# A decoder layer with product-key experts: all 128 lower tokens get their first products by gathered rows, 12 chunks of `u` are loaded beside the queries, and index look-ups go to 16 bits

## The chip, the cores and the metric

The kernel runs on one NeuronCore of a Trainium2 chip. The metric is the device time of one execution in microseconds (us), as the median over several runs. Engines are named as in the profile: PE is TensorE's matmul, PEld its weight load, DVE is VectorE, ACT is ScalarE, POOL is GpSimd, SP is SyncE, which here only issues transfers.

## The reference, cut to what matters

The layer normalises `x` (256 tokens of 1024), projects it, runs two attention branches, merges them and adds the result to `x`. Behind that stands the part that the change touches, PEER, a product-key expert retrieval. With `h2 = RMSNorm(x)` it computes, in words and symbols:

```
q      = h2 @ w_q                      # 8 heads, two halves of 128 each
s1, s2 = q halves @ sub_keys           # 128 scores each, per head
top 16 of s1, top 16 of s2             # 256 sums, of which the best 16 are kept
expert = 128 * i1 + i2                 # one of 16384
gate   = softmax(the 16 best sums)
out   += sum over 8 heads x 16 experts of gate * gelu(h2 . u[expert]) * v[expert]
```

`u` and `v` are tables of 16384 rows of 1024 float32 numbers, 64 MB each. A token uses 128 of the rows.

## The kernel before, in words

Tokens 128 to 255 (the upper ones) and part of the lower ones take their expert products densely: every row of `u` is multiplied with every such token, and a matrix of gates that is zero for experts not chosen selects. The other lower tokens have their 128 rows of `u` fetched by index and dotted on DVE.

**Projections.** All projections go through a list of pieces of 128x2x512 weights. SP loads them (`L191`) into a ring of 6 buffers, `raw_ring`; ACT (`L137`) and DVE (`L138`) cut each into a high and a low part, `rhi` and `rlo`; PE multiplies three combinations (`L219` to `L221`, `L228` to `L230`). The last 16 pieces are those of `w_q`, the queries stage. `pump()` advances the waiting epilogues by a step after each piece.

**Early turns.** While the projections run, `early_turns` loads a few chunks of `u` (a chunk is 128 rows), transposes them on DVE in blocks of 32 (`L682`) and stores them in DRAM as `turned`. `NPRE` of them, each eighth chunk, are later loaded ready-made; the others are transposed on PE (`L666`) and copied out by ACT (`L667`).

**The residual's epilogue** (`L510` to `L558`) makes `h2` and its transposes in `hTf`, of which `NA` columns are used. On POOL's queue it copies the rows of `NX` lower tokens to DRAM (`h2x`, `L553`), and from there to `h2y` (`L556`), where each row stands 8 times, once for each head. `h2r` tiles are loaded from `h2y` by `rows_x` at the start of the u stage.

**Queries.** `queries` (`L560`) evicts a piece's product (ACT `L564`), multiplies with the sub-keys (`L573`) and puts a `topk` generator on the chain. `topk` (`L821` to `L900`) runs on DVE in steps, paid from a budget (`BUDGET_Q` beside a piece, `BUDGET` beside a chunk). Its last part finds the expert numbers: a compare of `iota` with `tf` (`L853`), a multiply with `ce` (`L856`) and a reduce (`L857`), each over 128x864 numbers; then `ef` becomes `ei`, and the gates follow, normalised in `L889` to `L891`.

**The u stage** runs over 128 chunks (`L1122`): load of the next chunk on SP (`L621`, or `L642` for a turned one), transposes two chunks ahead, 8 matmuls against `hTf` of `NA` columns (`L1137`), and beside each chunk `GATHER` gather steps and a piece of the chain. A gather step fetches one row of `u` per partition by an indirect transfer on POOL (`L924`, four buffers) and dots the row that came three steps before on DVE (`dot_v`, `L935`). The first 64 of these are those of the 64 tokens that were always gathered (`h`), the other `NU` - 64 those of the `NX` extra tokens (16 for each of `NXG` groups, with `h2r` as the other operand). When the chain of the upper tokens is done, `dense_gates` (`L1040`) comes: `columns(1)` (`L1045`) transposes the indices and gates of the upper tokens on PE, then for four tokens at a time DVE makes one-hot rows (`L1025`, `L1026`), ACT scales them (`L1030`), PE multiplies (`gp`, `L1064`) and DVE and ACT write the result into `W` (`L1077`, `L1079`). `W` holds 128 chunks by `ND` = 192 tokens; its columns 0 to 87 (`SCRATCH`) serve as scratch or lie unused until the products arrive there.

**The V stage** (`L1174`) multiplies `W` with the table `v`, and gathers what belongs to the 64 tokens (`GATHER_V`).

All queues are in order, and the order is that in which the program is written. `load_to` issues a load on SP a fixed number of pieces or chunks ahead; a load waits until its ring buffer is free.

Of the kernel before, what the change touches and what calls it, by code (L numbers as in the profile page):

```python
# [11 lines left out]
F32 = mybir.dt.float32  # L12
F32R = mybir.dt.float32r
BF16 = mybir.dt.bfloat16
I32 = mybir.dt.int32
U32 = mybir.dt.uint32
AF = mybir.ActivationFunctionType
# [11 lines left out]
NG = 64  # L29
ND = S - NG  # L30
NXP = 16
NXG = 3
NX = NXP * NXG
NA = ND - NX
RING = 4
GATHER_V = 0.5
GATHER = 0.95
RAWS = 6
AHEAD = 4
TAHEAD = 2  # L40
# [3 lines left out]
LAG_G = 2  # L44
SCRATCH = 88
TOPK = 16
NPRE = 15
STEP = 8
PRE0 = 20
WARM = 8  # L50
# [14 lines left out]
def layer_kernel(ctx, tc, x, mix_norm_g, w_in, ret_w_branch, moba_q_gain, moba_k_gain, moba_w_branch,  # L65
# [444 lines left out]
    def residual(j):  # L510
        def epi(o):

            xg = []
            for t in range(NT):
                c = slice(512 * j, 512 * (j + 1))
                V.tensor_tensor(xt[:, t, c], xt[:, t, c], o[t], op=OP.add)
            for t in range(NT):
                c = slice(512 * j, 512 * (j + 1))
                a = t2([P, 512], "xg")
                V.tensor_tensor(a, xt[:, t, c], grow2[:, c], op=OP.mult)  # L520
                sq = t2([P, 512], "sq2")
                A.activation(sq, xt[:, t, c], AF.Square, accum_out=ss2[:, j, t:t + 1])
                xg.append(a)
            yield
            yield
            for t in range(NT):
                p = side()
                for c in range(4):
                    T.transpose(p[:, c * P:(c + 1) * P], xg[t][:, c * P:(c + 1) * P], ident)
                split_to(qk_h[j][:, :, t * P:(t + 1) * P], qk_l[j][:, :, t * P:(t + 1) * P],  # L530
                         p.rearrange("p (c q) -> p c q", c=4))
            if j == 0:
                return
            nc.gpsimd.dma_start(x1d, xt)  # L534
            V.tensor_tensor(ss2[:, 0], ss2[:, 0], ss2[:, 1], op=OP.add)
            V.tensor_scalar(ss2[:, 0], ss2[:, 0], 1.0 / D, EPS, op0=OP.mult, op1=OP.add)
            G.tensor_tensor(r2, ss2[:, 0], minus_half[:, :NT], op=OP.pow)
            yield
            V.scalar_tensor_tensor(h2, xt[:, 0, :], r2[:, 0:1], grow2, op0=OP.mult, op1=OP.mult)
            hn = t4([P, D], "hn2")  # L540
            V.scalar_tensor_tensor(hn, xt[:, 1, :], r2[:, 1:2], grow2, op0=OP.mult, op1=OP.mult)
            yield
            for src, t0, n0, n in ((h2, NG, P, NA - P), (hn, 0, 0, P)):
                for q in range(2):
                    k = slice(4 * q, 4 * q + 4)
                    p = side()
                    for c in range(4):
                        T.transpose(p[:, c * P:(c + 1) * P], src.rearrange("p (i k) -> p k i", k=KC)[:, 4 * q + c], ident)
                    pv = p.rearrange("p (c q) -> p c q", c=4)[:, :, t0:t0 + n]
                    A.activation(hTf[:, k, n0:n0 + n], pv, AF.Copy)  # L550
                yield

            nc.gpsimd.dma_start(h2x, h2[P - NX:])  # L553
            nc.gpsimd.dma_start(h2[NG:], h2[:NG])
            yield
            nc.gpsimd.dma_start(h2y, h2x.rearrange("(n i) d -> n i d", n=NXG)[:, None].to_broadcast([NXG, H, NXP, D]))  # L556
            yield
        return epi  # L558

    def queries(q):  # L560
# [67 lines left out]
    def load_any(i):  # L628
# [8 lines left out]
            load(i)  # L637
        elif i < len(pieces) + NK:
            c = i - len(pieces)
            if c % STEP == STEP - 1 and c // STEP < NPRE:  # L640
                u_raw[c] = raw_tile()
                nc.sync.dma_start(u_raw[c], turned[c // STEP])  # L642
            else:
                u_raw[c] = load_rows(peer_u, c)
        elif i < len(pieces) + 2 * NK:
            v_raw[i - len(pieces) - NK] = load_rows(peer_v, i - len(pieces) - NK)
# [174 lines left out]
    def topk(t, q, s_sb):  # L821
# [11 lines left out]
        cand = []  # L833
        for n0, src in ((6400, v), (6528, xf)):
            dst = scratch[:, n0:n0 + 2 * NCAND].rearrange("p (h n) -> p h n", h=2)
            for (i, a, b), n in zip(CAND, COFF):
                V.tensor_tensor(dst[:, :, n:n + a * b].rearrange("p h (a b) -> p h a b", a=a),
                                src[:, 1, :, None, :b].to_broadcast([P, 2, a, b]),
# [4 lines left out]
        ts_ = tk.tile([P, 2, TOPK], F32, name="ts_")  # L843
        ti = tk.tile([P, 2, TOPK], U32, name="ti")
        tf = tk.tile([P, 2, TOPK], F32, name="tf")
        ef = tk.tile([P, 2, TOPK], F32, name="ef")
        for _ in top16([(ts_[:, h, :], ti[:, h, :], cs[:, h, :], tmp[h][:, :NCAND]) for h in range(2)]):
            yield 0.55
        V.tensor_copy(tf, ti)
        yield 0.85  # L850
        for h in range(2):
            oh = scratch[:, 5120:5120 + TOPK * NCAND].rearrange("p (k n) -> p k n", k=TOPK)
            V.tensor_tensor(oh, iota[:, None, :NCAND].to_broadcast([P, TOPK, NCAND]),  # L853
                            tf[:, h, :, None].to_broadcast([P, TOPK, NCAND]), op=OP.is_equal)
            yield 0.9
            V.tensor_tensor(oh, oh, ce[:, h, None, :].to_broadcast([P, TOPK, NCAND]), op=OP.mult)  # L856
            V.tensor_reduce(ef[:, h, :], oh, axis=AX.X, op=OP.add)  # L857
            yield 1.9
        sl = slice(2 * q * TOPK, 2 * (q + 1) * TOPK)
        e1 = ef.rearrange("p h k -> p (h k)")  # L860
# [108 lines left out]
    def gather_step():  # L969
# [21 lines left out]
        if gs["sum"] < gs["v"] and (gs["v"] - gs["sum"] == RING or gs["v"] == NJ):  # L991
# [6 lines left out]
                V.scalar_tensor_tensor(gs["acc"], r, av[:, j:j + 1], gs["acc"], op0=OP.mult, op1=OP.add)  # L998
            gs["sum"] += 1

    for i in range(n_mixer + 3, len(pieces)):
        load_to(i + 1)
        cut(i + 3)
        products(i)
        pump()
# [1 line left out]

    while tasks:  # L1010
        pump()
    cps.close()
# [266 lines left out]
```

## Time and profile before

| | |
|---|---|
| median of 3 runs | 1034.11 us (1033.67 to 1040.05) |
| the profiled execution | 1033.85 us, its span 1031.8 us |
| granted TensorE clock, mean | 0.992 |
| PE busy | 1005.6 us, 97% of the span |
| DVE, ACT, POOL busy | 815.1, 546.1, 307.0 us |
| queries stage ends, u stage begins | about 332 us |
| DMA traffic | 301.43 MB, mean 292 GB/s |

The profile is one execution. A row of a list of waits says which engine at which line waited for what: us in total, times, longest. A row of the chain of waits gives a start, a duration and what the time went to. A row of a timeline gives start, duration, engine, line, operation, out<-in, and in brackets the idle time before. [...]

### The profile page before, as it was taken

The numbers are of one execution on the slowest core, as the hardware profiler recorded it, in microseconds if no ns is written. First come the engines' busy times: TensorE is split into PE (matmuls) and PEld (weight loads), VectorE is DVE, ScalarE is ACT, GpSimd is POOL, SyncE is SP. The second block draws the span as 40 slices with busy tenths as digits, with TensorE's granted clock in tenths as the row PEclk, the third lists the DMA queues.
The fourth block names the chain that finished last, engine by engine and source line by source line (L and its number), as shares of the span: only waits on it lengthen the run. The fifth ranks groups of instructions, "written<-read, shape, count | busy, mean of one in ns | idle before, by whom it ended". The sixth has DMA issues, their size and how long they took to land.

```text
span 1031.8 us, 19502 instructions
## 1 busy us (share of the span) xinstructions
PE 1005.6 (97%) x7384; PEld 967.9 (94%) x7384; DVE 815.1 (79%) x1482; ACT 546.1 (53%) x991; POOL 307.0 (30%) x256
## 2 busy tenths in 40 slices
PE   8999999999949999999999999999999999999997
PEld 6887998997949999999999999999999999999997
DVE  6567667978548895699977999994788888888887
ACT  5545544534524434443346776679655555555553
POOL 2421000000102344444443443542433333333330
PEclk9999999999969999999999999999999999999999
DMA  9775787987735999899999787887799999999993
GB/s 332 194 201 169 235 247 212 301 269 225 239 123 162 383 372 352 330 367 373 376 384 344 280 284 255 285 320 244 270 345 345 352 336 345 348 343 345 341 347 108
DMA packets 103067, 301.43 MB, mean 292 GB/s; under 512 B 10740, under 2 KB 21005, under 8 KB 102822
## 3 DMA queue, kind: packets, MB, share of 16 engines
q1 hardware_dynamic: 64732, 186.07, 52.1%
q0 software_dynamic: 27008, 96.82, 26.0%
q10 hardware_dynamic: 11234, 17.31, 5.4%
q8 instruction: 58, 0.95, 0.4%
q14 instruction: 35, 0.29, 0.1%
HBM read 289.15 MB, written 12.00 MB: 292 GB/s over the span
## 4 chain that ended last, share of the span: by engine, by line
PE 89%; DMA 3%; DVE 3%; ACT 2%; issue 1%; ACTq 0%; POOL 0%; DVEq 0%; POOLq 0%
PE acc L1137 24%; PE acc L1170 19%; PE turn L666 10%; PE acc L1171 8%; PE gp L1064 4%; PE acc L228 3%; PE acc L229 3%; PE acc L230 3%; PE acc L219 3%; PE acc L220 3%; PE acc L221 3%; DMA raw_ring<-in_peer_w_q_dram 2%; PE side L573 1%; PE side L349 1%; PE side L374 1%
## 5 line engine op out<-in xcount | busy, mean ns | idle before, releaser
L924 POOL DMA_INDIRECT rows<-in_peer_u_dram,eg x112 | 140.0, 1250 | 130.0 <-DVE rows L935 50.4
L924 POOL DMA_INDIRECT rows<-in_peer_v_dram,eg x64 | 106.8, 1669 | 168.3 <-DVE vacc L998 167.4
L666 PE MATMUL turn<-ident,raw_ring 128*128 128x128 f32 x904 | 118.5, 274 | 0.8 <-ACT W L577 0.8
L666 PEld LDWEIGHTS turn<-ident,raw_ring 128*128 128x128 f32 x904 | 110.0, 191 | 1.0 <-ACT W L577 1.0
L935 DVE SCALAR_TENSOR_TENSOR rows<-rows,h 128x1024 f32<-128x1024 f32 x64 | 78.4, 1229 | 8.6 <-DMA rows<-in_peer_u_dram,eg 8.5
L998 DVE SCALAR_TENSOR_TENSOR vacc<-rows,av,vacc 128x1024 f32<-128x1024 f32 x63 | 80.6, 1279 | 0.0
L1108 ACT ACTIVATE cw<-W 128x384 fp32r<-128x384 f32 x64 | 33.7, 526 | 81.9 <-PE acc L1171 31.7
L1109 DVE TENSOR_TENSOR cw<-W,cw 128x384 fp32r<-128x384 f32 x64 | 36.3, 568 | 33.7 <-ACT cw L1108 33.7
L1079 ACT ACTIVATE W<-gp 128x512 f32<-128x512 f32 (+18 forms) x48 | 27.5, 577 | 41.4 <-DVE W L1077 35.0
L1030 ACT ACTIVATE oh_buf<-oh_buf,tT 128x128 f32<-128x128 f32 x128 | 40.9, 407 | 0.4 <-DVE oh_buf L1026 0.4
L1077 DVE TENSOR_TENSOR W<-gp,W 128x328 f32<-128x328 f32 (+17 forms) x36 | 36.5, 1015 | 5.3 <-PE gp L1064 5.0
L1094 POOL TENSOR_TENSOR W<-W,gl 128x288 f32<-128x288 f32 (+17 forms) x24 | 15.6, 651 | 83.9 <-ACT gl L1093 77.8
L935 DVE SCALAR_TENSOR_TENSOR rows<-rows,rlo__3191 128x1024 f32<-128x1024 f32 x16 | 19.4, 1217 | 21.1 <-DMA rows<-in_peer_u_dram,eg 21.0
L1064 PE MATMUL gp<-oh_buf 128*128 128x128 f32 x256 | 33.8, 276 | 0.0
L1137 PE MATMUL acc<-hTf,raw_ring 128*128 128x144 f32 x240 | 31.9, 286 | 0.0
L1064 PEld LDWEIGHTS gp<-oh_buf 128*128 128x128 f32 x256 | 31.5, 191 | 0.1
L1137 PEld LDWEIGHTS acc<-hTf,raw_ring 128*128 128x128 f32 x240 | 30.3, 190 | 0.0
L534 POOL DMA_DIRECT2D x1d<-xt x1 | 0.7, 652 | 91.7 <-DMA raw_ring<-in_peer_w_q_dram 91.7
L1025 DVE TENSOR_TENSOR oh_buf<-niota,tT 128x512 f32<-128x512 f32 x32 | 22.1, 690 | 7.0 <-PE gp L1064 6.4
L144 POOL TENSOR_TENSOR gny<-va,minus_half 128x8 f32<-128x8 f32 x2 | 3.3, 1653 | 79.1 <-DVE va L436 79.1
L935 DVE SCALAR_TENSOR_TENSOR rows<-rows,rlo__3252 128x1024 f32<-128x1024 f32 x16 | 19.3, 1218 | 9.4 <-DMA rows<-in_peer_u_dram,eg 9.4
L1026 DVE TENSOR_TENSOR oh_buf<-iota,tT 128x512 f32<-128x512 f32 x32 | 25.4, 793 | 0.0
(2091 smaller groups left out, 3491.2 us busy)
## 6 DMA issues: line engine op xcount, KB each, us to landing
raw_ring<-in_peer_v_dram SPq DMA_DIRECT2D x128, 512.0 KB
raw_ring<-in_peer_u_dram SPq DMA_DIRECT2D x113, 512.0 KB
raw_ring<-in_w_in_dram SPq DMA_DIRECT2D x52, 512.0 KB
raw_ring<-in_peer_w_q_dram SPq DMA_DIRECT2D x16, 512.0 KB
raw_ring<-turned SPq DMA_DIRECT2D x15, 512.0 KB
eraw<-in_peer_u_dram ACTq DMA_DIRECT2D x32, 128.0 KB
turned<-eT ACTq DMA_DIRECT2D x8, 512.0 KB
raw_ring<-in_ret_w_branch_dram SPq DMA_DIRECT2D x8, 512.0 KB
```

The lines of the kernel that those rows point to most:

```text
L666: T.transpose(p[:, k * P:(k + 1) * P], r.rearrange("p (i k) -> p k i", k=KC)[:, 4 * q + k], ident)
L924: G.indirect_dma_start(out=r, out_offset=None, in_=tab, in_offset=bass.IndirectOffsetOnAxis(ap=eg[:, j:j + 1], axis=0))
L935: V.scalar_tensor_tensor(r, r, 1.0, h, op0=OP.mult, op1=OP.mult, accum_out=av[:, j:j + 1])
L998: V.scalar_tensor_tensor(gs["acc"], r, av[:, j:j + 1], gs["acc"], op0=OP.mult, op1=OP.add)
L1030: A.activation(o1[:, j], o1[:, j], AF.Copy, scale=tT[:, t, 2, k + j:k + j + 1])
L1064: T.matmul(p[:, j * P:(j + 1) * P], o2, o1, start=True, stop=True)
L1077: V.tensor_tensor(w[:, :, :c], p[:, :, :c], w[:, :, :c], op=OP.mult)
L1108: A.activation(w[:, :, :ND], W[:, c:c + 2, :], AF.Copy)
L1109: V.tensor_tensor(w[:, :, ND:], W[:, c:c + 2, :], w[:, :, :ND].bitcast(F32), op=OP.subtract)
L1137: T.matmul(pa[:, n:n + NA], uT[:, k * P:(k + 1) * P], hTf[:, k], start=(c % 2 == 0 and k == 0), stop=(k == KC - 1), skip_group_check=True)
L1170: T.matmul(o[b][:, :2 * ND], vh[:, n], w, start=(c == 0), stop=False, skip_group_check=True)
L1171: T.matmul(o[b][:, :ND], vl[:, n], w[:, :ND], start=False, stop=(c == NK - 1), skip_group_check=True)
```

## The change

Five edits. `NXG` goes from 3 to 4, so all lower tokens gather their first products: `NX` 48 to 64, `NU` 112 to 128, `NA` 144 to 128 columns of `L1137`, and `GATHER` 0.95 to 1.08. Twelve chunks of `u` (0, 1, 2, 8, 14, ... 56) are loaded by `hold` beside the queries' pieces into unused columns of `W`, and `load_any` skips them later. `h2y` is written by four copies with 16 rows outermost instead of one copy with 24. The expert look-up's `ce`, `oh` and `ef` become 16-bit integers. `NPRE` goes from 15 to 14. The rest of the text keeps the line numbers of the kernel before; in the changed kernel they are a few higher.

```diff
-NXG = 3
+NXG = 4
 NX = NXP * NXG
 NA = ND - NX
...
-GATHER = 0.95
+GATHER = 1.08
...
-NPRE = 15
+HELD = [0, 1, 2] + list(range(8, 62, 6))
+HELD0 = 20
+NPRE = 14
...
             for src, t0, n0, n in ((h2, NG, P, NA - P), (hn, 0, 0, P)):
-                for q in range(2):
+                for q in range(2 if n else 0):
...
-            nc.gpsimd.dma_start(h2y, h2x.rearrange("(n i) d -> n i d", n=NXG)[:, None].to_broadcast([NXG, H, NXP, D]))
-            yield
+            for n in range(NXG):
+                src = h2x[NXP * n:NXP * (n + 1)]
+                nc.gpsimd.dma_start(h2y[n].rearrange("h i d -> i h d"), src[:, None, :].to_broadcast([NXP, H, D]))
+                yield
...
             c = i - len(pieces)
+            if c in HELD:
+                return
...
             dst = scratch[:, n0:n0 + 2 * NCAND].rearrange("p (h n) -> p h n", h=2)
+            if src is xf:
+                dst = tk.tile([P, 2, NCAND], I16, name="ce", bufs=2)
...
-        ef = tk.tile([P, 2, TOPK], F32, name="ef")
+        ef = tk.tile([P, 2, TOPK], I16, name="ef")
...
-            oh = scratch[:, 5120:5120 + TOPK * NCAND].rearrange("p (k n) -> p k n", k=TOPK)
+            oh = scratch[:, 5120:5120 + TOPK * NCAND // 2].bitcast(I16).rearrange("p (k n) -> p k n", k=TOPK)
...
+    def hold():
+        n0, c = 1024 * (len(HELD) - len(held)), held.pop(0)
+        u_raw[c] = W[:, HELD0:SCRATCH, :].rearrange("p c t -> p (c t)")[:, n0:n0 + D]
+        nc.sync.dma_start(u_raw[c], peer_u[0, c * P:(c + 1) * P, :])
+
     for i in range(n_mixer + 3, len(pieces)):
         load_to(i + 1)
+        if held and i > n_mixer + 3:
+            hold()
...
+    while held:
+        hold()
```

On SP's queue the queries stage stood so before: the loads of `w_q`, with two of the sub-keys between, then the first chunks of `u`.

```order
L191 DMA raw_ring<-in_w_out_dram 128x2x512 x8
L191 DMA raw_ring<-in_peer_w_q_dram 128x2x512 x5
L632 DMA raw_ring<-in_peer_sub_keys_dram 128x8x128 x2
L191 DMA raw_ring<-in_peer_w_q_dram 128x2x512 x11
L621 DMA raw_ring<-in_peer_u_dram 128x1024 x7
L642 DMA raw_ring<-turned 128x1024
```

After the change, from the sub-keys on (`L1016` is `hold`; the lines left out alternate one `w_q` load and one held load):

```order
L637 DMA raw_ring<-in_peer_sub_keys_dram 128x8x128 x2
L194 DMA raw_ring<-in_peer_w_q_dram 128x2x512 x4
L1016 DMA W<-in_peer_u_dram 128x1024
L194 DMA raw_ring<-in_peer_w_q_dram 128x2x512
...
L1016 DMA W<-in_peer_u_dram 128x1024 x4
L626 DMA raw_ring<-in_peer_u_dram 128x1024
L1016 DMA W<-in_peer_u_dram 128x1024
L626 DMA raw_ring<-in_peer_u_dram 128x1024 x3
L649 DMA raw_ring<-turned 128x1024
```

Of the last seven `w_q` loads each has a held load ahead of it, and five more held loads stand behind, among the first chunks; the ring's first three chunks fall away, since chunks 0 to 2 are held.

POOL's queue around the residual's epilogue, before:

```order
L534 DMA x1d<-xt 128x2048
L537 TENSOR_TENSOR r_75<-ss_116,minus_half 128x2
L553 DMA h2x<-h_74 48x1024
L554 DMA h_74<-h_74 64x1024
L556 DMA h2y<-h2x 24x1x16384
L867 DMA eg<-ei 64x16
L924 DMA rows<-in_peer_u_dram,eg 128x1024 x5
```

and in the changed kernel:

```order
L537 DMA x1d<-xt 128x2048
L540 TENSOR_TENSOR r_75<-ss_116,minus_half 128x2
L556 DMA h2x<-h_74 64x1024
L557 DMA h_74<-h_74 64x1024
L561 DMA h2y<-h2x 16x8x1024 x4
L877 DMA eg<-ei 64x16
L934 DMA rows<-in_peer_u_dram,eg 128x1024 x6
```

The one copy of 24 runs of 16384 numbers becomes four of 16x8 runs of 1024, and one gather more stands before the next copy of indices.

DVE just before the second `L891`, the end of the upper tokens' chain, before (`rlo__3252` is the third `h2r`, and `rows` is a gathered row):

```order
L853 TENSOR_TENSOR W<-iota,tf 128x864
L856 TENSOR_TENSOR W<-W 128x864
L857 TENSOR_REDUCE ef<-W 128x16
L935 SCALAR_TENSOR_TENSOR rows,av<-rows,rlo__3252 128x1024 x2
...
L879 TENSOR_TENSOR gates<-ts__5209 128x32
L935 SCALAR_TENSOR_TENSOR rows,av<-rows,rlo__3252 128x1024 x5
L889 TENSOR_REDUCE sm<-gates 128x8
L890 RECIPROCAL sm<-sm 128x8
L891 TENSOR_TENSOR gates<-gates,sm 128x128
```

and after (`rlo__3277` is the fourth `h2r`):

```order
L862 TENSOR_TENSOR W<-iota,tf 128x864
L865 TENSOR_TENSOR W<-W,ce 128x864
L867 TENSOR_REDUCE ef<-W 128x16
L945 SCALAR_TENSOR_TENSOR rows,av<-rows,rlo__3249 128x1024 x2
...
L889 TENSOR_TENSOR gates<-ts__5232 128x32
L945 SCALAR_TENSOR_TENSOR rows,av<-rows,rlo__3249 128x1024 x2
L945 SCALAR_TENSOR_TENSOR rows,av<-rows,rlo__3277 128x1024 x4
L899 TENSOR_REDUCE sm<-gates 128x8
L900 RECIPROCAL sm<-sm 128x8
L901 TENSOR_TENSOR gates<-gates,sm 128x128
```

One more dot stands in this stretch; over the whole stage 80 dots stand ahead of this last line, where there were 70. On PE `columns(1)` stays where it was, behind the products of 79 chunks.

## Rows read from the trace of the kernel before

**Rows 1.** The page: span, and busy time of each engine (busy us, share, instructions).

```profile
span 1031.8 us, 19502 instructions
PE 1005.6 (97%) x7384; PEld 967.9 (94%) x7384; DVE 815.1 (79%) x1482; ACT 546.1 (53%) x991; POOL 307.0 (30%) x256
```

**Rows 2.** The list of PE's waits from 0 to 340 us, its largest item.

```profile
PE side L573 <- ACT W L564: 13.1, 1, 13.1
```

**Rows 3.** ACT's timeline at 295.75 us, and the chain of waits from 275 us on (start, us, what). Between 302.47 and 304.60 stand eleven matmuls of 0.21 us.

```profile
295.75 1.06 ACT L137 ACTIVATE rhi__2735<-raw_ring 128x1024 fp32r<-128x1024 f32 x1 [15.16 <-DMA raw_ring<-in_peer_w_q_dram]
...
275.24 21.74 DMA raw_ring<-in_peer_w_q_dram
...
298.68 3.78 PE side L573 x16
302.47 0.21 PE acc L228
...
304.60 0.21 PE acc L229
...
305.93 0.12 PE acc L230
...
315.08 0.71 PE side L573 x4
315.79 1.60 PE side L573 x12
```

**Rows 4.** Windows of 4 us in the queries stage.

```profile
core 0: us, PE busy (x) PEld busy (x) DVE busy (x) ACT busy (x) POOL busy (x), PEclk, DMA share, GB/s
...
282.00:286.00 4.00, 3.62 (x31) 3.42 (x29) 0.17 (x1) 0.00 (x0) 0.00 (x0) 1.00 0.35 144
286.00:290.00 4.00, 0.00 (x0) 0.00 (x0) 0.00 (x0) 0.00 (x0) 0.00 (x0) 0.71 0.14 55
290.00:294.00 4.00, 0.00 (x0) 0.00 (x0) 0.00 (x0) 0.00 (x0) 0.00 (x0) 0.50 0.26 84
294.00:298.00 4.00, 0.00 (x0) 0.00 (x0) 1.16 (x2) 1.97 (x2) 0.00 (x0) 0.50 0.43 160
```

**Rows 5.** DMA queues from 286 to 294 us: packets, MB, share of 16 engines.

```profile
q0 software_dynamic: 8, 0.39, 11.7%
```

**Rows 6.** Windows of the u stage (columns as in rows 4).

```profile
332.00:397.00 65.00, 64.97 (x546) 64.97 (x547) 58.68 (x199) 28.40 (x56) 26.84 (x25) 1.00 0.98 377
397.00:433.00 36.00, 36.00 (x305) 36.00 (x305) 14.46 (x51) 17.94 (x33) 14.88 (x19) 1.00 0.85 310
433.00:532.00 99.00, 99.00 (x834) 99.00 (x833) 94.98 (x326) 39.27 (x81) 41.82 (x35) 1.00 0.99 378
532.00:550.00 18.00, 18.00 (x153) 18.00 (x152) 8.50 (x19) 10.44 (x19) 7.83 (x8) 1.00 1.00 387
550.00:690.00 140.00, 140.00 (x1198) 140.00 (x1198) 132.87 (x193) 99.30 (x301) 62.16 (x58) 1.00 0.82 293
```

**Rows 7.** Lists of the waits of DVE and of POOL from 335 to 550 us, the largest of each.

```profile
DVE rows L935 <- DMA rows<-in_peer_u_dram,eg: 38.6, 18, 10.7
...
POOL rows L924 <- DVE rows L935: 50.4, 26, 5.0
```

**Rows 8.** DMA from 332 to 550 us, all packets.

```profile
DMA packets 22272, 80.02 MB, mean 367 GB/s; under 512 B 2669, under 2 KB 2829, under 8 KB 22247
```

**Rows 9.** Timelines of DVE (first two rows) and PE (last row) around 546 us.

```profile
544.83 1.23 DVE L935 SCALAR_TENSOR_TENSOR rows<-rows,rlo__3252 128x1024 f32<-128x1024 f32 x1 [1.39 <-DMA rows<-in_peer_u_dram,eg]
...
546.53 0.29 DVE L891 TENSOR_TENSOR gates<-gates,sm 128x128 f32<-128x128 f32 x1
...
550.19 0.38 PE L1045 MATMUL turn<-ident,i12f 128*128 128x128 f32 x2
```

**Rows 10.** The view of the one line `L682`: count, shortest/median/longest in ns, and the longest wait for it.

```profile
L682 DVE STREAM_TRANSPOSE eT<-eraw x16: 1107/1156/1218, 82.5 to 238.8; 128x512 f32<-128x512 f32 x16
...
  ACT rhi__1677 L137: 2.1, 1
```

**Rows 11.** The chain of waits in the u stage, before the gates (first two) and in the gate part (last).

```profile
503.68 0.89 PE turn L666 x8
504.57 1.96 PE acc L1137 x16
...
560.12 0.89 PE gp L1064 x8
```

**Rows 12.** Groups of DVE instructions by line from 332 to 728 us (count | busy us, mean ns of one), and the first dot's row of DVE's timeline.

```profile
L935 DVE SCALAR_TENSOR_TENSOR rows<-rows,rlo__3252 128x1024 f32<-128x1024 f32 x16 | 19.3, 1218 | 9.4 <-DMA rows<-in_peer_u_dram,eg 9.4
L1077 DVE TENSOR_TENSOR W<-gp,W 128x328 f32<-128x328 f32 (+17 forms) x36 | 36.5, 1015 | 5.3 <-PE gp L1064 5.0
L857 DVE TENSOR_REDUCE ef<-W 128x16 f32<-128x864 f32 x14 | 14.7, 1053 | 0.5
L856 DVE TENSOR_TENSOR W<-W 128x864 f32<-128x864 f32 x13 | 13.7, 1056 | 0.2
L837 DVE TENSOR_TENSOR W<-txf 128x16 f32<-128x16 f32 (+3 forms) x30 | 3.3, 177 | 0.0
...
335.59 1.22 DVE L935 SCALAR_TENSOR_TENSOR rows<-rows,h 128x1024 f32<-128x1024 f32 x1
```

**Rows 13.** Windows of DVE's `L935` alone: length, DVE busy (x counts two records for each dot), PEclk, DMA share, GB/s.

```profile
433.00:532.00 99.00, 43.76 (x72) 1.00 0.99 378
```

More of the change, by code (lines that the diff above doesn't have):

```diff
@@ L14 @@
 BF16 = mybir.dt.bfloat16
+I16 = mybir.dt.int16
 I32 = mybir.dt.int32
@@ L856, in topk @@
             V.tensor_tensor(oh, oh, ce[:, h, None, :].to_broadcast([P, TOPK, NCAND]), op=OP.mult)
-            V.tensor_reduce(ef[:, h, :], oh, axis=AX.X, op=OP.add)
+            with nc.allow_low_precision("one term of each sum is not zero, an integer below 2 ** 14"):
+                V.tensor_reduce(ef[:, h, :], oh, axis=AX.X, op=OP.add)
             yield 1.9
@@ L999, in gather_step @@
             gs["sum"] += 1
+    held = list(HELD)
+    def hold():
+        n0, c = 1024 * (len(HELD) - len(held)), held.pop(0)
+        u_raw[c] = W[:, HELD0:SCRATCH, :].rearrange("p c t -> p (c t)")[:, n0:n0 + D]
+        nc.sync.dma_start(u_raw[c], peer_u[0, c * P:(c + 1) * P, :])
     for i in range(n_mixer + 3, len(pieces)):
         load_to(i + 1)
+        if held and i > n_mixer + 3:
+            hold()
         cut(i + 3)
```

## The prediction

> **What bounds the kernel now.** The page comes first: TensorE is busy for 1005.6 of a span of 1031.8 us [rows 1]. So time can go only where PE's own work shrinks or where PE waits. The list of PE's waits up to the end of the queries stage holds one large item, 13.1 us for ACT's `L564` [rows 2]. From 332 to 690 us PE is busy in every us of every window at a granted clock of 1.00 [rows 6]: the u stage is bound by PE's instructions.
>
> The stall, followed back: ACT's cut `L137` sat 15.16 us until a piece of `w_q` landed, and the chain of waits has that transfer from 275.24 on, for 21.74 us [rows 3]. Meanwhile the DMA engines were mostly idle: shares 0.35, 0.14, 0.26, 0.43 in the four windows from 282 us [rows 4]. What ran between 286 and 294 us was on POOL's queue, q0: 8 packets, 0.39 MB, 11.7% of the engines [rows 5], some 49 KB a packet. That is `h2y<-h2x`, whose rows of 16384 elements are 64 KB each. My reading: the `w_q` load is spread over all engines and is done only when its last part is, and a few engines sit behind long packets. The stall also costs clock: granted 0.50 from 290 to 298 us [rows 4]. The first `L573` group behind it took 3.78 us where the next took 0.71 + 1.60, and 11 matmuls took 0.21 instead of 0.12 [rows 3]: 1.5 + 1.0 = 2.5 us.
>
> In the u stage DVE and POOL have waits that PE does not see: DVE 38.6 us for gathered rows, POOL 50.4 for DVE to free a row buffer [rows 7]. The DMA engines stand at 0.98 to 1.00 there save in one stretch at 0.85 [rows 6], moving 80.02 MB from 332 to 550 at a mean of 367 GB/s [rows 8]. That matters because of one meeting point: PE's `columns(1)` (`L1045`) transposes `i12f` and `gates`, which the last DVE `L891` of the token half completes. DVE ended it at 546.53 + 0.29 = 546.82; PE came at 550.19 and did not wait [rows 9]. The slack is 3.4 us. An edit that makes PE earlier by more than that turns into a wait, unless DVE gets there earlier too.
>
> **The change, part by part.** The sum is made against the profiled run's own 1033.85 us, 0.3 below the median of 1034.11.
>
> *Early turns, 15 to 14.* One pair of DVE transposes of 1156 ns goes, and with it a wait like the 2.1 us that ACT spent on one [rows 10]; PE is paced there by the cuts. Between 0 and -2; I take -1.0. Chunk 119 is then turned on PE: 8 transposes, 0.89 us [rows 11], +0.9.
>
> *Row copies.* Four copies of 16x8x1024 put 4 KB packets on 16 rows. If they spread, the stall goes: -13.1, with its clock -2.5. Bounds 0 to -15.6. [...]
>
> *Held loads.* 12 loads of 0.524 MB are 6.3 MB, at 387 GB/s [rows 6] 16.3 us of DMA time, interleaved on SP with the `w_q` loads. Between 282 and 298 us the engines have room for about 70% of that [rows 4], and `w_q` itself would land earlier. Bounds 0 to +16 (all in front of the pieces that PE needs); I take +1, as the engines' free share is the nearest row.
>
> *Short matmuls.* A chunk's 16 steps take 1.96 us with 144 moving columns; 16 `gp` steps with 128 columns of the same type take 2 x 0.89 = 1.78 [rows 11]. That is -0.18 a chunk, x128 = -23.0. PE has no idle time to absorb it. Upper bound 0, if another engine paces the stage.
>
> *All lower tokens gathered.* 16 more rows and 16 more dots `L935` of 1.22 us [rows 12] on DVE. By the order of instructions 80 u dots, where 70 stood, come before the `L891` that PE waits for, while `columns(1)` stays behind 79 chunks. PE gets there 79 x 0.18 = 14.2 us sooner in the stage: 550.19 - 332.03 = 218.2 becomes 204. DVE got there at 214.8. What will it need now? By bytes: 12 loads less are -6.3 MB, 10 or 11 rows more +5.5, one more `h2r` +0.5: the same 80 MB through engines that were full. So about 215 again; at the 387 GB/s of the best window all the way it is 207, and I allow 222 for later row buffers. **A new wait of PE, 215 - 204 = 11 us** (3 to 18), and behind it the same clock loss as behind the 13.1: +2.5.
>
> *Gate part (550 to 690).* DVE is busy for 132.87 of 140 [rows 6]. GATHER 1.08 adds 0.13 x 38 chunks = 5 dots, 6 us; 32 evictions `L1077` of 1015 ns instead of 36 [rows 12] take 4 back, and PE's steps get 0.18 us shorter while DVE's work a step does not. +3, between 0 and +6.
>
> *16 bits.* The multiply costs 1056 ns and the reduce 1053, 13 and 14 of them after 332 us [rows 12]. No row has them in 16 bits. Nearest below is an elementwise operation on 128x16, 177 ns [rows 12]; a conversion could cost as much again. So a gain of 0 to 0.88 us each; I take 0 for the sum. Whatever it saves first lengthens DVE's wait for rows (cover 38.6 us); without that cover the 13 multiplies at half time would be 6.9 us. [...]
>
> Sum: 1033.85 - 1.0 + 0.9 - 13.1 - 2.5 + 1.0 - 23.0 + 11.0 + 2.5 + 3.0 = 1012.7, **1013 us**. With the wait between 3 and 18, own range 1005 to 1020.
>
> **The rivals.**
> A. *DVE keeps up, no wait at `columns(1)`*: 1013 - 13.5 = 999. For it: the stretch at DMA share 0.85 is slack, and the held chunks lie at the front, where they let the gathers run ahead. Against it: POOL and DVE wait on each other there [rows 7], and the engines are full otherwise.
> B. *The gathers keep their pace per dot.* The first dot began at 335.59, the 70th at 544.83 [rows 9, 12]: 209.24 / 69 = 3.03 us each. 80 of them then end the chain at 3.6 + 79 x 3.03 + 2.0 = 245 us, the wait is 41, and the time 1013 + 30 = 1043, slower than before. It decides at 2.92 us a dot, where the wait is 32. For it: the ring of four row buffers and POOL's 50.4 us. Against: from 433 to 532 us 36 dots took 99 us, 2.75 each [rows 13], and those had more chunk loads beside them.
> C. *The stall stays in another form*: small copies that are mostly overhead, or held loads ahead of `w_q`. +15.6: 1028. For it: 6.3 MB are added to the very window. Against: the idle shares.
> D. *The 16-bit multiplies run at half time and DVE is the bound*: 13 x 0.53 = 6.9 us off the new wait, and the clock loss stays: 1006. Against: DVE waits for rows, so its time is not what ends last.
>
> **How the numbers follow.** Chances: the forecast 0.46, A 0.18, B 0.09, C 0.12, D 0.10, others 0.05. The likeliest gives 1013. The range runs from 997 (A, with a gate part at 0 instead of +3) to 1032 (C with the longer wait); outside lie B and a tail of A, under 2 in 10. One per cent, 10.3 us, is about what a measurement can tell from no change: 1023.8 and 1044.5 are the bounds. The forecast, A and D are faster, 0.74, less a few hundredths for a wait near 20 us and half of the others: 0.69. C and most of B lie within 1%: 0.26. Slower is B's upper half: 0.05.
>
> **What would show it.** Right: no `L573` wait above 2 us, the windows 282 to 298 with shares near 1; 16 `L1137` steps in 1.78; a PE wait of about 11 us at `columns(1)` on `gates`; an unchanged 0.98 DMA share up to it. Wrong: PE waiting at `u` loads instead (held chunks late, or gathers crowding them), a wait for `w_q` of 10 us or more, or `L856` still at 1.05 with DVE as the last to end. A result under 1003 means A; one above 1025 means B or C, told apart by where PE waits.

## The result, and the profile after

The changed kernel takes 1029.38 us, the median of 20 runs, against 1034.17 us before: a ratio of 0.9947, with an interval of 0.9929 to 0.9965. That is half a per cent faster, where 2% had been forecast (1013 us, range 997 to 1032). The profiled execution took 1025.9 us. Its runs scatter from 1022 to 1033 us, those of before from 1032 to 1040; two of the changed kernel's, at 1040 and 1041 us, more than 1.5% above its fastest, are left out of this range and of the ratio.

The page's first lines, and PE's list of waits over the whole span (us in total, times, longest):

```profile
span 1024.1 us, 19561 instructions
PE 989.0 (97%) x7384; PEld 950.7 (93%) x7384; DVE 822.9 (80%) x1508; ACT 547.3 (53%) x989; POOL 319.8 (31%) x278
...
PE acc L1158 <- ACT rhi__5491 L674: 12.7, 1, 12.7
PE gp L1085 <- ACT oh_buf L1051: 4.1, 5, 1.6
PE turn L1066 <- DVE gates L901: 3.6, 1, 3.6
PE side L578 <- ACT W L569: 2.5, 2, 2.2
```

PE's busy time fell by 16.6 us [rows 1]. The stall in the queries stage went from 13.1 [rows 2] to 2.5 us in two waits, the longer of 2.2, and a new one of 12.7 + 3.6 us stands in the u stage. First the queries stage, in windows of 4 us (columns as in rows 4: busy us of each engine and its instructions, TensorE's granted clock as a share of full speed, the mean busy share of the 16 DMA engines, GB/s):

```profile
278.00:282.00 4.00, 4.00 (x36) 4.00 (x35) 3.11 (x15) 1.06 (x1) 0.00 (x0) 1.00 1.01 392
282.00:286.00 4.00, 1.85 (x13) 1.64 (x12) 3.33 (x17) 2.03 (x3) 0.00 (x0) 0.92 1.04 405
286.00:290.00 4.00, 4.00 (x26) 4.00 (x25) 1.09 (x11) 1.87 (x3) 0.00 (x0) 0.66 1.04 396
```

The DMA engines stand at 1.01 to 1.04 where they stood at 0.14 to 0.43 [rows 4]. The u stage begins at the first transpose of a held chunk, 317.6 us, and not at 332.0:

```profile
L673 PE MATMUL turn<-ident,W x96: 272/274/375, 317.6 to 458.5; 128*128 128x128 f32 x96
```

Now the new stall. ACT's timeline shows where PE's wait of 12.7 us comes from: ACT reached the `Exp` of the upper tokens' gates (`L896`) and stood 16.67 us for DVE's `L889` there, and the copies `L674` of transposed chunks, which PE needs, are queued behind it.

```profile
511.46 1.28 ACT L896 ACT_TABLE_LOAD   x1
529.41 0.31 ACT L896 ACTIVATE gates<-gates 128x128 f32<-128x128 f32 x1 [16.67 <-DVE gates L889]
529.63 1.07 ACT L674 ACTIVATE rhi__5491<-turn 128x512 f32<-128x512 f32 x2
```

The chain of waits goes on from there to `columns(1)` and out into the gate part:

```profile
519.65 7.61 DMA rows<-in_peer_u_dram,eg
...
527.29 1.23 DVE rows L945 x2
...
529.63 0.95 POOL rows L934
...
532.87 5.78 DMA rows<-in_peer_u_dram,eg
...
538.74 1.23 DVE rows L945 x2
...
540.44 0.30 DVE gates L901
...
540.78 0.33 PE turn L1066
541.11 1.42 PE turn L673 x8
542.53 2.90 PE acc L1158 x16
...
549.87 1.79 PE acc L1158 x16
```

This is a loop: a row lands, DVE dots it, the free buffer lets POOL issue the next row, and that one lands 6 to 8 us later. The norm `L901` ends at 540.74, which is 223.1 us behind the stage's start (214.8 before, [rows 9]). And 16 matmuls take 1.79 us, not 1.96 [rows 11]. PE's clock shows what the wait cost besides:

```profile
522.00:526.00 4.00, 0.00 (x0) 0.00 (x0) 3.75 (x5) 0.00 (x0) 2.45 (x2) 0.50 1.03 409
526.00:530.00 4.00, 0.00 (x0) 0.00 (x0) 3.86 (x11) 0.59 (x2) 2.17 (x2) 0.50 0.53 206
530.00:534.00 4.00, 3.74 (x17) 3.74 (x18) 2.90 (x6) 3.34 (x6) 3.39 (x3) 0.50 0.85 264
534.00:538.00 4.00, 3.21 (x27) 2.97 (x25) 2.17 (x3) 1.36 (x3) 2.33 (x3) 0.94 0.87 290
538.00:542.00 4.00, 1.22 (x8) 1.22 (x9) 3.50 (x10) 0.72 (x2) 1.87 (x2) 0.92 0.89 338
542.00:546.00 4.00, 4.00 (x26) 4.00 (x25) 3.90 (x8) 2.32 (x7) 2.95 (x3) 0.66 0.72 231
```

PE's timeline has the first 16 matmuls behind the wait of 12.7 us take 3.78 us, where the 16 ahead of it took 1.95, and the 8 transposes after them 1.37 and not 1.05, which is 2.15 us lost. Behind the second wait the chain above shows 1.42 and 2.90 us for what later takes 0.89 (8 transposes) and 1.79, another 1.64.

From `columns(1)` to the first matmul of the V stage 182.0 us pass, where it was 178.8 before. The V stage itself takes 301.3 and 302.6 us.

### The profile page after: what moved, and what is told of

It reads as the page before. It is cut to its first block, busy times and chain, and to the rows that moved or that the text cites. A ratio compares the mean times of both kernels' runs of the same rounds, so it can differ in the third digit from the quotient of the medians.

```text
span 1024.1 us, 19561 instructions
## 1 busy us (share of the span) xinstructions
PE 989.0 (97%) x7384; PEld 950.7 (93%) x7384; DVE 822.9 (80%) x1508; ACT 547.3 (53%) x989; POOL 319.8 (31%) x278
## 4 chain that ended last, share of the span: by engine, by line
PE 60%; DMA 14%; DVE 12%; issue 6%; POOL 4%; ACT 3%; POOLq 0%; DVEq 0%; SPq 0%; ACTq 0%
PE acc L1191 20%; DMA rows<-in_peer_u_dram,eg 11%; PE acc L1192 9%; DVE rows L945 5%; PE acc L231 4%; PE acc L233 4%; PE acc L232 4%; PE acc L222 4%; PE acc L223 3%; PE acc L224 3%; POOL rows L934 3%; PE acc L1158 3%; PE gp L1085 1%; DVE W L1098 1%; PE turn L673 1%
## 5 line engine op out<-in xcount | busy, mean ns | idle before, releaser
L934 POOL DMA_INDIRECT rows<-in_peer_u_dram,eg x128 | 150.7, 1177 | 127.4 <-DVE rows L945 50.1
L934 POOL DMA_INDIRECT rows<-in_peer_v_dram,eg x64 | 102.4, 1599 | 170.3 <-DVE vacc L1008 164.8
L673 PE MATMUL turn<-ident,raw_ring 128*128 128x128 f32 x816 | 108.2, 276 | 0.7 <-ACT rhi__6709 L674 0.7
L673 PEld LDWEIGHTS turn<-ident,raw_ring 128*128 128x128 f32 x816 | 99.5, 191 | 0.9 <-ACT rhi__6709 L674 0.9
L1100 ACT ACTIVATE W<-gp 128x512 f32<-128x512 f32 (+16 forms) x48 | 30.7, 643 | 36.1 <-DVE W L1098 32.9
L1115 POOL TENSOR_TENSOR W<-W,gl 128x256 f32<-128x256 f32 (+15 forms) x24 | 17.9, 746 | 79.3 <-ACT gl L1114 73.1
L1098 DVE TENSOR_TENSOR W<-gp,W 128x328 f32<-128x328 f32 (+15 forms) x32 | 31.8, 993 | 0.9 <-PE gp L1085 0.5
L1158 PE MATMUL acc<-hTf,raw_ring 128*128 128x128 f32 x224 | 28.5, 282 | 0.0
L1158 PEld LDWEIGHTS acc<-hTf,raw_ring 128*128 128x128 f32 x224 | 27.4, 200 | 0.0
```

What stands on the lines that cost most here:

```text
L673: T.transpose(p[:, k * P:(k + 1) * P], r.rearrange("p (i k) -> p k i", k=KC)[:, 4 * q + k], ident)
L934: G.indirect_dma_start(out=r, out_offset=None, in_=tab, in_offset=bass.IndirectOffsetOnAxis(ap=eg[:, j:j + 1], axis=0))
L1098: V.tensor_tensor(w[:, :, :c], p[:, :, :c], w[:, :, :c], op=OP.mult)
L1158: T.matmul(pa[:, n:n + NA], uT[:, k * P:(k + 1) * P], hTf[:, k], start=(c % 2 == 0 and k == 0), stop=(k == KC - 1), skip_group_check=True)
```

## The experiments

"Chain end" is the end of the second `L901` (in the kernel before `L891`), counted from the first transpose of the u stage: 214.8 us before, 223.1 in the whole change. Times are medians. Edits are against the changed kernel.

**Without the fourth group.**

```diff
-NXG = 4
+NXG = 3
-GATHER = 1.08
+GATHER = 0.95
```

> The change without its fourth group of gathered tokens: NXG 3 and GATHER 0.95 as before, so 144 columns and 70 dots ahead of the upper tokens' last norm, with the held chunks, the small copies, the 16-bit look-ups and NPRE 14 kept. Theory S (supply: in the u stage the gathered rows come through full DMA engines, the chain of the upper tokens ends when its rows have landed, and the whole gain of the short matmuls is handed back as PE's wait and as a DVE-bound gate part): the front keeps its 14.4 us, no wait at the Exp or at columns(1), PE's pitch stays at 1.96 for 16 matmuls; 1018 to 1021 us, so faster than the whole change at 1029. Theory F (the fourth group still pays on balance, some 5 to 10 us, and the loss lies elsewhere): slower than the whole change, 1034 to 1039.

Measured: 1016.71 us, ratio 0.9836 (0.9823 to 0.985); chain end 209.4, no wait there. So the other four edits alone bring 17 us, and the fourth group, as it was put in, costs 12.7 us on balance. Theory F falls; S's time was 1.3 us too high.

**No held chunks.**

```diff
-HELD = [0, 1, 2] + list(range(8, 62, 6))
+HELD = []
```

> The whole change with no held chunk: all 12 are loaded in the u stage again, which puts 6.3 MB more ahead of columns(1). Theory S: the upper tokens' chain ends 15 to 18 us later behind the stage's start (at 357 GB/s), PE's wait there grows from 16 to 30 us or more, and the time is 1040 to 1047 us. Theory D (DVE's own work and the hand-over of four row buffers set the end of the chain, not bytes): the wait stays at 16 us and the time at 1027 to 1031. In both the queries stage keeps its gain, or gains 1 to 2 us.

Measured: 1037.36 us, ratio 1.004 (1.0024 to 1.0055); chain end 232.3, and PE waits 21.2 + 2.9 us. The 6.3 MB matter, but for 9 us and not for the 15 to 18 that bytes over a full engine would give. Theory D falls, and S is too strong.

**GATHER back at 0.95.**

```diff
-GATHER_V = 0.5
+GATHER_V = 0.7
-GATHER = 1.08
+GATHER = 0.95
```

> The whole change with GATHER back at 0.95, so 70 dots instead of 80 stand ahead of the upper tokens' last norm, and about 10 of the 64 tokens' own rows are dotted in the V stage, whose GATHER_V goes from 0.5 to 0.7 to take them in. Theory S: 5.2 MB less ahead of columns(1), the chain ends about 208 us behind the stage's start where PE comes at 204, the wait is 0 to 5 us, the clock is not lost, and the time is 1008 to 1016 us. If the gate part is what DVE bounds whatever stands ahead of it (theory G): the wait goes but the gate part grows, 1020 to 1027.

Measured: 1002.36 us (996.9 to 1003.3), ratio 0.9694 (0.9681 to 0.9707). Chain end 206.8, PE waits 1.0 us for it, and the part from there to the V stage takes 172.0 us and not 182.0. Ten dots fewer ahead of the norm are worth 27 us, more than S had said, since the gate part recovers too.

**Half of each chunk loaded.**

```diff
-        nc.sync.dma_start(r, tab[0, c * P:(c + 1) * P, :])
+        n = P // 2 if tab is peer_u else P
+        nc.sync.dma_start(r[:n], tab[0, c * P:c * P + n, :])
```

> The whole change with each chunk of u that is loaded into the ring in the u stage cut to its first 64 rows; the other half of the buffer keeps old numbers, so the products of half the experts are left out. Instructions on every engine stay the same; 15 MB less ahead of columns(1). Theory S: the chain ends near 181 to 195 us behind the stage's start, no wait of PE at the Exp or at columns(1), and 1006 to 1013 us. Theory D: DVE is busy for 181 us of its 223 there whatever the loads do and the row buffers go round as before, the wait stays above 10 us, 1024 to 1030.

Measured: 1060.75 us, ratio 1.026 (1.0227 to 1.0293), chain end 252.8: both expectations missed. The DMA queues from 340 to 520 us (packets, MB, share of 16 engines), of this run, and then of the whole change:

```profile
q0 software_dynamic: 8147, 28.20, 54.8%
q1 hardware_dynamic: 5315, 17.92, 39.7%
```

```profile
q0 software_dynamic: 9445, 32.94, 48.5%
q1 hardware_dynamic: 8766, 31.94, 45.7%
```

A packet on q1 took on average 0.397 x 16 x 180 us / 5315 = 215 ns, against 0.457 x 16 x 180 / 8766 = 150; on q0 194 against 148. With loads into 64 partitions the mean packet of both queues was slower in this run, those of the rows too; why, no run shows. As a test of bytes the run is spoilt; it does show that PE's wait (35.2 us) follows the rows' landing with DVE's instructions unchanged.

**Odd chunks not loaded.** The clean form of the same test.

```diff
+            elif c % 2 and c - 1 in u_raw and c - 1 not in HELD:
+                u_raw[c] = u_raw[c - 1]
```

> The whole change, but of two neighbouring chunks of u the odd one is not loaded where its even neighbour was: it takes the neighbour's buffer, so its experts' products are wrong and 11.5 MB (22 chunks of 128 whole rows) are missing ahead of columns(1). Unlike the cut to 64 rows, where each 4 KB packet took some 215 ns in place of 150, the packets stay as they are. Theory S (bytes over full DMA engines set when the upper tokens' chain ends): it ends 191 to 200 us behind the stage's start, PE does not wait, 1005 to 1012 us. Theory D (DVE's own work sets it): the end stays at 220 or more, 1026 to 1031. Theory M (the first 60 us are DVE's, the rest is supply): 205 to 213, a wait of 2 to 8 us, 1011 to 1020.

Measured: 1011.83 us, ratio 0.9786 (0.9768 to 0.9804); chain end 216.2, PE waits 5.6 + 3.9 us. The DMA engines stood at 0.92 in the stage's first 62 us, at 0.77 in the next 40 and at 0.93 to 0.94 in the 100 behind, so they had room, and still the chain ended only 7 us sooner. S and D fall.

**Half dots.**

```diff
-        V.scalar_tensor_tensor(r, r, 1.0, h, ...
+        V.scalar_tensor_tensor(r[:, :D // 2], r[:, :D // 2], 1.0, h[:, :D // 2], ...
```

> The whole change with each dot of a gathered row over 512 of its 1024 numbers: half of each first product of the lower tokens is left out, and a dot takes some 0.69 us in place of 1.22. Bytes and the order are the same. Theory S: the chain still ends 215 to 223 us behind the stage's start, the wait of PE there is 11 us or more, and only the gate part gains: 1018 to 1026. Theory D: 80 dots less 0.53 us are 42 us, the chain ends well before PE, 1002 to 1009. Theory M: the end at 205 to 214, 1008 to 1017.

Measured: 1011.71 us, ratio 0.9793 (0.9774 to 0.9813); chain end 216.1, PE waits 5.9 + 2.6 us. So 11.5 MB less and 30 us of DVE's work less (it is busy for 133.7 of the stage's first 202 us, and for 163.8 in the whole change) are worth the same 7 us of the chain's end. Neither resource alone sets it. DVE's waits for rows grew from 36.4 to 65.2 us in those 202 us: most of what the dots gave up went into waiting. M named these times, but put the chain's end 2 to 3 us too early, and its reason, one bound after the other, does not fit: each relief helps a little. My reading is that of a loop whose steps follow one another; it led to theory L below.

**Look-ups in 32 bits.**

```diff
-            if src is xf:
-                dst = tk.tile([P, 2, NCAND], I16, name="ce", bufs=2)
-        ef = tk.tile([P, 2, TOPK], I16, name="ef")
+        ef = tk.tile([P, 2, TOPK], F32, name="ef")
...
-            oh = scratch[:, 5120:5120 + TOPK * NCAND // 2].bitcast(I16)...
+            oh = scratch[:, 5120:5120 + TOPK * NCAND]...
```

> The whole change with the look-ups in 32 bits as before; the multiply then takes 1056 ns again and not 607, 13 to 14 times in the u stage, 6 us in all, most of them ahead of the upper tokens' norm. Theory S: DVE waits that much less for rows, the chain ends where it did, 1027 to 1031. Theory D: 5 to 6 us later, 1033 to 1036.

Measured: 1034.83 us (12 runs), ratio 1.0007 (0.999 to 1.0024); chain end 232.4. Against the change's 1029.38 that is 5.4 us, as theory D had it: the look-ups' time (13 x 0.449 = 5.8 us) comes through although DVE waits for rows for 36.4 us of the stage's first 202 in the change and for 38.1 here. In the whole change the multiply takes 607 ns in place of 1056 [rows 12], and the reduce is as it was:

```profile
L867 DVE TENSOR_REDUCE ef<-W 128x16 int16<-128x864 int16 x14 | 14.7, 1053 | 0.5
...
L865 DVE TENSOR_TENSOR W<-W,ce 128x864 int16<-128x864 int16 x13 | 7.9, 607 | 0.2
```

**One copy for `h2y`.**

```diff
-            for n in range(NXG):
-                src = h2x[NXP * n:NXP * (n + 1)]
-                nc.gpsimd.dma_start(h2y[n].rearrange("h i d -> i h d"), src[:, None, :]...
-                yield
+            nc.gpsimd.dma_start(h2y, h2x.rearrange("(n i) d -> n i d", n=NXG)[:, None]...
+            yield
```

> The whole change with h2y written by one copy again, now of 32 runs of 16384 numbers. If the 64 KB packets on few DMA engines were what held up w_q: the stall at the sub-keys' products comes back with 13 us or more and its clock loss, the u stage starts 14 to 20 us later, 1043 to 1050. If the held loads or the order of the queue had removed it: 1027 to 1032.

Measured: 1046.17 us, ratio 1.014 (1.0112 to 1.0169). The old stall is back at its old size, and the u stage begins at 328.9 us:

```profile
PE side L576 <- ACT W L567: 13.1, 1, 13.1
```

So the form of the copies removed it; without the held chunks it stayed away as well (u stage at 315.0). The packets in the trace show which form: in this run 32 packets of 64 KB follow one another four at a time, most of them 2.4 us long, and in the kernel before 24 of them three at a time. That is as many side by side as there are groups (`NXG`), so my reading is that the groups stand outermost in the one copy, and not its 24 or 32 runs. The four copies changed two things at once, the 4 KB packets and the 16 rows outermost; no run tells them apart.

**A fifth row buffer.** `tk`, a pool of tiles, has room for one.

```diff
-RING = 4
+RING = 5
...
-        tag = "hh" if j % 2 else "hl"
-        r = hp_.tile([P, D], F32, name="rows", tag=tag, bufs=2)
+        n = gs["n"] = gs.get("n", -1) + 1
+        tag = ("hh", "hl", "hh", "hl", "r5")[n % 5]
+        r = tk.tile([P, D], F32, name="rows", tag=tag) if tag == "r5" else hp_.tile(...)
```

> The whole change with a fifth row buffer, so that four gathered rows are on their way where there were three. Nothing else changes but that a dot comes one gather step later (79 in place of 80 ahead of the norm). Theory L (loop: a row takes some 8.0 to 8.3 us from issue to landing, three are out, so a row comes each 2.8 us; this, and neither bytes nor DVE alone, sets the end of the upper tokens' chain): the pace falls to 2.5 to 2.6 us a row, held there by the DMA engines, the chain ends 203 to 213 us behind the stage's start, PE waits 0 to 7 us, 1004 to 1016. Theory S (the engines are full, so one more row on its way only waits longer): from issue to landing 10 to 11 us, the end at 218 or later, 1024 to 1031.

Measured: 1006.37 us, ratio 0.974 (0.9712 to 0.9767); chain end 206.8, PE waits 2.3 us. L holds: 23 us for one buffer, with the same bytes to move and one dot fewer ahead of the norm. In the profiled run the V stage is 5.7 us longer than in the change (307.1 us, PE waits 4.1 us for DVE near its end), so it begins 26 us sooner there (696.5 against 722.8). Windows of the u stage's first 182 us (columns as in rows 4), of the whole change and then of this run:

```profile
317.60:379.60 62.00, 61.96 (x556) 61.96 (x557) 53.94 (x192) 28.53 (x58) 27.37 (x24) 1.00 0.94 359
379.60:419.60 40.00, 40.00 (x362) 40.00 (x361) 21.13 (x65) 19.75 (x39) 16.42 (x23) 1.00 0.83 303
419.60:459.60 40.00, 40.00 (x362) 40.00 (x361) 34.20 (x131) 17.25 (x36) 16.77 (x17) 1.00 1.00 383
459.60:499.60 40.00, 40.00 (x362) 40.00 (x361) 35.69 (x108) 16.41 (x35) 17.07 (x16) 1.00 0.99 382
```

```profile
316.40:378.40 62.00, 61.96 (x556) 61.97 (x557) 59.47 (x204) 28.53 (x58) 32.86 (x29) 1.00 1.00 386
378.40:418.40 40.00, 40.00 (x362) 40.00 (x361) 25.07 (x92) 19.74 (x39) 18.94 (x25) 1.00 0.94 344
418.40:458.40 40.00, 40.00 (x362) 40.00 (x361) 38.29 (x128) 17.26 (x36) 21.72 (x18) 1.00 0.98 381
458.40:498.40 40.00, 40.00 (x362) 40.00 (x361) 38.95 (x154) 16.41 (x35) 16.56 (x16) 1.00 1.01 397
```

So the fifth buffer gained mostly where four had left the DMA engines room: in the first 102 us 37 dots had begun where there were 33. In the next 80 us, at a share of about 1.00 in both, it was 32 dots and 30, and 389 GB/s against 383. That full engines take more is not shown.

**Three row buffers.**

```diff
-RING = 4
+RING = 3
...
-        tag = "hh" if j % 2 else "hl"
-        r = hp_.tile([P, D], F32, name="rows", tag=tag, bufs=2)
+        n = gs["n"] = gs.get("n", -1) + 1
+        if n == 0:
+            gs["ring"] = [hp_.tile([P, D], F32, name="rows", tag=tag, bufs=2) for tag in ("hh", "hl", "hh")]
+        r = gs["ring"][n % 3]
```

> The whole change with three row buffers in place of four (a dot comes one gather step sooner, 81 ahead of the norm), as the counter-check to the fifth buffer, which took the pace from 2.89 to 2.60 us a row and 23 us off the time. Theory L (a row's way from issue over landing and dot to the next issue, shared by the buffers): about one row less on its way of the 2.8 that are there on average, somewhat quicker to land as less is asked for, so 3.3 to 3.7 us a row; the chain ends 265 to 295 us behind the stage's start, PE waits 50 us or more, 1070 to 1105. Theory S (supply): no change, 1026 to 1032.

Measured: 1084.17 us, ratio 1.0486 (1.0463 to 1.0509). The chain end is 253.7, PE waits 40.5 + 6.2 us; the pace counted by issues is in L's range, while the chain's end, the wait and the pace up to that end come out better than it. Theory S falls. Issues of rows in the first 204 us of the u stage (count, and the median us from issue to landing where the view has it), with three, four and five buffers:

```profile
rows<-in_peer_u_dram,eg POOLq DMA_INDIRECT x61, 7.4
```

```profile
rows<-in_peer_u_dram,eg POOLq DMA_INDIRECT x70
```

```profile
rows<-in_peer_u_dram,eg POOLq DMA_INDIRECT x80, 8.4
```

That is 204 / 61 = 3.34, 2.91 and 2.55 us a row. From the first dot to the last one ahead of the norm it is 3.15 us (81 dots), 2.80 (80) and 2.59 (79). On its way was a mean of 61 x 7.4 / 204 = 2.2 of three rows, and 80 x 8.4 / 204 = 3.3 of five.

**GATHER 0.95 with five buffers.** `fetch` as with the fifth buffer above.

```diff
-GATHER_V = 0.5
+GATHER_V = 0.7
-GATHER = 1.08
+GATHER = 0.95
-RING = 4
+RING = 5
```

> GATHER 0.95 and GATHER_V 0.7 together with the fifth row buffer. There is no wait of PE left to take away, as PE is busy for 980.7 of 995.1 us with GATHER 0.95 alone: both theories expect 998 to 1003, no more than 3 us from that run's 1002.4. Below 997 would mean that the rows still held PE up somewhere.

Measured: 993.86 us (993.45 to 996.14), ratio 0.9617 (0.9599 to 0.9636): the best version, 40 us under the kernel before. The chain ends 196.3 us behind the stage's start, 8 us ahead of PE. By the median it gains 8.5 us over four buffers and lies under the 997 that had been named as the sign that rows still held PE up; by the profiled runs it gains 3.4, since that of four buffers was the fastest of its five. The other four runs with four buffers fit that sign: their granted clock was 0.994 to 0.996, that of the profiled one 1.00.

**GATHER 0.95 without held chunks.**

```diff
-GATHER_V = 0.5
+GATHER_V = 0.7
-GATHER = 1.08
+GATHER = 0.95
-HELD = [0, 1, 2] + list(range(8, 62, 6))
+HELD = []
```

> GATHER 0.95 and GATHER_V 0.7 without the 12 held chunks. With 80 dots the held chunks were worth 9 us of the chain's end and 8 us of time. Theory L: the end comes 7 to 9 us later than 207 behind the stage's start, PE waits 9 to 12 us, its clock falls, 1011 to 1018. If the held chunks matter only where the rows are the bound anyway: 1001 to 1006.

Measured: 1003.41 us, ratio 0.9712 (0.9687 to 0.9738) against 1002.36 with them. Its profile has the chain end 5.7 us later (212.5) and a wait of 6.3 us at `columns(1)`, so the medians and the two profiles don't agree on what the held chunks are worth there. Its granted clock, 0.994 to 0.996, is that of the four slower runs with held chunks, so PE may have waited in those as well; no profile of one shows it, and that stays open.

## Why the prediction was wrong, step by step

1029.4 us lies inside the outer range of 997 to 1032, and that is luck: its upper end was rival C's with the longer wait, and C's condition did not come true. The forecast's own range was 1005 to 1020.

**The front was right.** -1.0 - 13.1 - 2.5 + 1.0 = -15.6 had been forecast; the u stage begins 14.4 us sooner in the profiled run, and 15 to 18 us sooner in the experiments that kept the small copies. The cause lies in the form of the copies, as named: with one copy and its 64 KB packets, four at a time and most of them 2.4 us long, the 13.1 us are back, and with the four copies they are gone. That a few engines sat behind those packets stays a reading; no run shows the engine of a packet. The small terms were not tested apart, save that without the held chunks the stage began 2.7 us sooner, where +1.0 had been taken.

**The short matmuls were right.** 1.79 us for 16, and the whole -23.0: between three groups (1016.71) and four groups with neither stall nor late rows (993.86) lie 22.9 us.

**The step that failed is "by bytes ... so about 215 again".** It took the DMA engines for full because they stood at 0.98 to 1.00 [rows 6], and the sum left out the stretch at 0.85, though it had been named as slack for rival A. The bytes came as forecast, 79.7 MB up to the chain's end where 80 had been said; the rate did not. From 317.6 to 541 us of the changed kernel, all packets:

```profile
DMA packets 22242, 79.66 MB, mean 357 GB/s; under 512 B 2700, under 2 KB 2860, under 8 KB 22219
```

80 MB in 215 us would be 372 GB/s. In the stage's first 102 us the engines stood at 0.94 and 0.83. The chain ended 223.1 us behind the stage's start, beyond the 222 that the range of the wait allowed, and PE waited 16.3 us in place of 11, which the range of 3 to 18 holds. What the runs show in its place is the ring: a row's buffer is taken from POOL's issue over the landing (a median of 7.4 us with three buffers, 8.4 with five) and the dot (1.22 us), which stands in DVE's order behind steps of `topk`, to the next issue. The pace hangs on the number of buffers (3.34, 2.91, 2.55 us a row, at a mean of 338, 362 and 381 GB/s) and gives a little to everything that shortens the way: fewer bytes beside it, shorter dots, faster look-ups (7, 7 and 9 us of the chain's end in the profiled runs). Rival B had this mechanism and the ring as its reason, at a chance of 0.09; its price was too high, because it kept 3.03 us a row, where the 80 dots came at 2.80; in the profiled runs the held chunks and the 16 bits each took 9 us off the chain's end (223 against 232 without the one or the other, and the change's profiled run lies 3.5 us under its median). The rows to see it in were there: POOL's 50.4 us behind DVE and DVE's 38.6 us for rows [rows 7] in the same stretch, two engines that wait for each other in turn.

**Where PE waits** was named as `columns(1)`. It waited first, 12.7 of the 16.3 us, for ACT, which stood at the `Exp` ahead of it in the program. The size is hardly changed by that: `columns(1)` came 223.1 us behind the stage's start where 204 had been forecast for a PE that does not wait (with five buffers and GATHER 0.95 it came at 204.3), and the 16.3 us of waiting with the 2.15 us of slow clock ahead of it fill those 19 us.

**The gate part** was put at +3, and +2.5 for the clock. It took 182.0 us. 178.8 less 8.8 (49 chunks at 0.18) and with 0.9 for chunk 119 would be 170.9, so it cost 11.1 us and not 5.5. The clock behind the second wait is 1.6 us of that; ahead of `columns(1)` it cost 2.15, so 3.8 us in all where +2.5 had been put. The number of dots is not the cause: with five buffers and the same GATHER it took 173.2 us. DVE waits there 13.6 us for rows with four buffers, and 4.4 with five:

```profile
DVE rows L945 <- DMA rows<-in_peer_u_dram,eg: 13.6, 11, 3.2
```

```profile
DVE rows L946 <- DMA rows<-in_peer_u_dram,eg: 4.4, 5, 1.4
```

**The 16 bits** were taken at 0, with DVE's wait for rows as cover. They are worth 5.4 us, so they hid a part of the miss: with the look-ups in 32 bits the whole change takes 1034.8 us, 22 above the forecast. The cover did not hold for them; my reading is that the next row is then asked for later too. It is no rule: of the 30 us that the half dots took from DVE only 7 reached the chain's end. Rival D had the size (6.9) and was argued away with that cover. Its half time was an assumption that no run shows: in the change's trace the multiply takes 607 ns in place of 1056, a factor of 1.74 and not 2, and the reduce 1053 as before.

In numbers, for the profiled runs, forecast against measured: front -15.6 and -14.4; `columns(1)` behind the stage's start -3.2 and +4.7; the rest up to the V stage -2.4 and +3.2; V stage 0 and -1.3. The sums are -21.2 and, with rounding, -7.9. The median lies another 3.5 us above the profiled run; with the end hanging on when rows land, runs scatter over 11 us, against 1 to 3 in the versions where PE does not wait for them (1016.41 to 1017.32 without the fourth group).

## What to carry to other kernels

Where two engines wait for each other in turn and a ring of buffers lies between them, count the buffers before the bytes: pace is the way of one item, from issue back to issue, over the items on their way (here 3.34, 2.91 and 2.55 us a row with three, four and five buffers). Read the share of the DMA engines stage by stage before calling them full: here 0.94 and 0.83 stood ahead of windows at 0.99 to 1.00, and a fifth buffer made 1.00 and 0.94 of them. Do not count on a wait inside such a loop to hide work: 5.8 us of look-ups came through whole, 30 us of dots in small part. And when an edit takes work off the bounding engine, ask at its next meeting point with the others what their chain needs by then: here ten dots more ahead of it turned a gain of 23 us into a loss of 13, and one more buffer, with those dots put behind it, gave all of it.

## What the runs showed of the hardware

Three things were not expected. With loads into 64 of the 128 partitions the mean time of a packet rose on both queues, the gathered rows' too, from about 150 to 194 and 215 ns, and with half of each chunk's bytes the kernel took 31 us longer than with all of them. One more row on its way raised the issues of rows by 14% (70 to 80 in 204 us) and the mean rate from 362 to 381 GB/s, nearly all of it in stretches where the 16 DMA engines had stood at 0.83 to 0.94; where they stood at 1.00 the rate went from 383 to 389. And PE stood idle from 517.6 to 530.3 us, and its granted clock was 0.50 from 522 to 534; it rose to 0.94, was 0.66 behind the second wait and 1.00 from 546 us on. The work done at the lower clock cost 3.8 us more, beside 16.3 us of waiting.
